# A decoder layer's projection stage with a third h buffer and norms ahead, and FFN norm sums moved from TensorE to GpSimd

## The chip, the cores and the metric

The kernel runs on the 8 cores of one Trainium2 chip, as one program on each. The metric is device time in microseconds (us) of the slowest core. A run is called slow when one die of four cores shows a lower granted TensorE clock and is over 1% longer than the other, or when it is over 1.5% above the fastest run of its kernel. Such runs happened to most kernels here (2755 to 3060 us) and are left out: all comparisons are of fast runs.

The four cores numbered 0 to 3 are die 0, the others die 1. Engines in the profile's words: PE is TensorE (PEld its weight loads), DVE is VectorE, ACT is ScalarE, POOL is GpSimd, SP is SyncE, whose queue issues most transfers. PSUM is the memory that TensorE writes its results to; another engine has to empty it. DMA stands for transfers.

## The reference

One layer: RMSNorm, one input projection, a convolution branch and a forgetting attention branch, a shared output projection, post-norm and residual, then a SwiGLU FFN with a norm before and behind it. Four sequences of 8192 tokens, width 1024, FFN width 2816.

```python
h = rmsnorm(x, g_mix_pre)
a_val, a_gate, q, k, v, f_logit = split(h @ w_in)
u = a_val * sigmoid(a_gate)                         # GLU, 512 channels
conv_out = silu(layernorm(causal_depthwise_conv(u, conv_w, conv_b)))   # width 31
log_f = log_sigmoid(f_logit + b_forget)
attn_out = forgetting_attention(q, k, v, log_f)     # causal, 8 heads x 64
mix = concat([conv_out, attn_out]) @ w_out
x = x + rmsnorm(mix, g_mix_post)
h = rmsnorm(x, g_ffn_pre)
y = (silu(h @ w_gate) * (h @ w_up)) @ w_down
x = x + rmsnorm(y, g_ffn_post)
```

Two cores share a sequence. Each computes k, v and forget logits for all 16 chunks of 512 tokens, and q, convolution, output and FFN for its own 8 chunks, the odd ones in its own numbering. Tensors are transposed: channels on partitions, tokens along the row.

## The kernel before

The program is written by Python generators. The "filler" (projection, then FFN) yields after every few matmuls; at each yield one deferred step of each waiting list is issued (`tick`), and a share of attention work is put in. In the traces each engine's work comes in the order written, so a matmul written ahead of another is also ahead of it there.

```python
# one buffer for all input weights; a part is a row block, so every load writes all 8 parts
win = BP("win", [128, 8, DIN], BF16, parts=8)
...
def wl(name, lo, hi, n=1):
    ...  # DMA with cast: out=win[:, :, lo:hi],
         # writes=[("winp", name)] + win.keys[...]   -> each load waits for the one before
wl("k", C_K, C_V); wl("v", C_V, DIN); wl("gv", 0, C_Q); wl("q", C_Q, C_K)
...
def p_chunk(i):                                      # (cut) one projection chunk
    own, j, H = i % 2 == 1, i // 2, hT[i % 2]        # two h buffers
    load_x(i + 1)
    K: 4 x 8 matmuls -> kst, deferred store to k_s;  V: 4 x 8 -> vst, deferred store to v_s
    squares of x(i+1) on ACT (deferred); forget logits
    if even:  conv_mm(j - 1), with norm_stats(i + 1) inside; conv_ln(j - 1)
    else:     Q; norm_stats(i + 1); gates: 4 x (GATE, VAL) -> u -> u_s in DRAM;
              then load u back as u4, four shifted copies (deferred)
    cvt_some(2)          # 2 of 30 conversions of FFN weights, DRAM to DRAM, f32 to bf16
...
def stats(src, nk, b, ...):                          # sum of squares over channels:
    nk matmuls of ones_bf by bf16 squares            # nk = 8 for every RMSNorm
def A2(j):                                           # norm behind the output projection
    yield from stats(sqf, 8, b); norm_tail(...)      # Ln and Exp on ACT give rstd
    defer("x1", [resid(mix, V_GPOST, X, ob) for ob in range(8)])       # DVE
    defer("x1", [square(X, sqf, ob) for ob in range(8)], 3)            # ACT
def A3(j):                                           # norm before the FFN
    flush("x1"); yield from stats(sqf, 8, b); norm_tail(...)
    defer("h2", [scale_by(x1[j % 2], V_GFPRE, rstdf, h2, k) for k in range(8)])
def N2(j): ...                                       # norm behind the FFN, same form
...
def f_stream():                                      # (cut) FFN; chunk j+1's norms inside chunk j
    f_load(0); f_loadx(0)
    A1(0); conv_mm(7); A2(0); conv_ln(7); A3(0); flush("ln")
    for j in range(8):
        11 up groups (32 matmuls each): N2(j-1) behind group 0; behind group 4, attention of
        chunk j+1 must be done; A1(j+1) behind groups 6 to 9
        8 down blocks (22 matmuls each): A2(j+1) ahead of block 0, A3(j+1) ahead of block 3
```

The softmax here doesn't subtract the row's maximum and nothing guards it: scores larger than these inputs give would overflow.

Of the kernel before, what the change touches and what calls it, by code (L numbers as in the profile page):

```python
# [10 lines left out]
D = 1024  # L11
# [182 lines left out]
def build_program():  # L194
# [66 lines left out]
    win = BP("win", [128, 8, DIN], BF16, parts=8)  # L261
    xs = BP("xs", [128, 8, CH], F32, parts=8)
    hT = [BP(f"hT{i}", [128, 8, CH], BF16, parts=8) for i in range(2)]
# [3 lines left out]
    rt = BP("rt", [128, CH], F32)  # L267
    rstd = BP("rstd", [128, CH], F32)
    w4 = BP("w4", [128, 8, 16, 32], BF16)
    u4 = BP("u4", [128, 16, WIN], BF16, planes=4)  # L270
    ust = [BP(f"ust{i}", [128, CH], BF16) for i in range(2)]
    th = [BP(f"th{i}", [128, CH], F32) for i in range(2)]
    acc = BP("acc", [128, 4, CH], F32, parts=4)
    lsq = BP("lsq", [128, 8, CH], BF16, parts=8)
    mean = BP("mean", [128, CH], F32)
    m2 = BP("m2", [128, CH], F32)
    lrt = BP("lrt", [128, CH], F32)
    lrs = BP("lrs", [128, CH], F32)
    lth = [BP(f"lth{i}", [128, CH], F32) for i in range(2)]
    cvst = [BP(f"cvst{i}", [128, CH], BF16) for i in range(2)]  # L280
    kmask = BP("kmask", [128, 4], F32)
# [3 lines left out]
    tot = BP("tot", [128, 32], F32)  # L285
# [6 lines left out]
    sq = BP("sq", [128, 8, CH], BF16, parts=8)  # L292

    fc = [base]
    BF_ = lambda name, shape, dt, parts=1: Buf(name, shape, dt, parts, fc)
    mix = BF_("mix", [128, 8, CH], F32, parts=8)
    x1 = [None, None]
    x1[0] = BF_("x1_0", [128, 8, CH], F32, parts=8)
    h2 = BF_("h2", [128, 8, CH], BF16, parts=8)
    fc[0] = max(fc[0], xs.off)  # L300
    at = BF_("at", [128, 4, CH], BF16)
    cv = BF_("cv", [128, 4, CH], BF16)
    sqf = BF_("sqf", [128, 8, CH], BF16, parts=8)
    fc[0] = max(fc[0], hT[0].off)
    wr = [BF_(f"wr{i}", [128, 2048], BF16) for i in range(NWR)]
    rtf = BF_("rtf", [128, CH], F32)
    rstdf = BF_("rstdf", [128, CH], F32)
    tmp = [BF_(f"tmp{i}", [128, CH], F32) for i in range(2)]
    actT = BF_("actT", [128, NFB, CH], BF16, parts=NFB)
    x1[1] = BF_("x1_1", [128, 8, CH], F32, parts=8)  # L310
    thf = [BF_(f"thf{i}", [128, CH], F32) for i in range(2)]
    sa = [BF_(f"sa{i}", [128, CH], F32) for i in range(2)]
    sqy = BF_("sqy", [128, 8, CH], BF16, parts=8)
    assert fc[0] <= sq.off
    fc[0] = max(fc[0], sq.off)
    wout = BF_("wout", [128, 8, D], BF16)
# [49 lines left out]
    def norm_tail(b, rtb, rstdb, scale, ncol=CH):  # L366
        P.op("act", lambda e: e.activation(out=rtb[:, 0:ncol], in_=pb[b][:, 0:ncol], func=AF.Ln, bias=epsb[:, 0:1], scale=scale),  # L367
             reads=[PB(b)] + epsb.keys, writes=rtb.keys)
        P.op("act", lambda e: e.activation(out=rstdb[:, 0:ncol], in_=rtb[:, 0:ncol], func=AF.Exp, scale=-0.5),
             reads=rtb.keys, writes=rstdb.keys)  # L370

    def stats(src, nk, b, ncol=CH, k0=0):
        yield from group(nk, lambda k: ones_bf[:], lambda k: src[:, k0 + k, 0:ncol], pb[b][:, 0:ncol],
                         lambda k: ones_bf.keys + [src.keys[k0 + k]], b, cost=ncol / 2400.0)
# [17 lines left out]
    def load_x(i):  # L392
        for g in range(4):
            ld("sp", xs, xs[:, 2 * g:2 * g + 2, :], xT_d[i, :, 2 * g:2 * g + 2, :], keys=xs.keys[2 * g:2 * g + 2], sem=("xs", g))

    def square(src, dst, k):
        return lambda: P.op("act", lambda e: e.activation(out=dst[:, k, :], in_=src[:, k, :], func=AF.Square),  # L397
                            reads=[src.keys[k]], writes=[dst.keys[k]])
# [6 lines left out]
    wkey = lambda k, c: [("winp", c)]  # L405

    def proj_T(H, c0, b, wk):
        yield from group(8, lambda k: win[:, k, c0:c0 + 128], lambda k: H[:, k, :], pb[b][:],
                         lambda k: [("winp", wk), win.keys[k], H.keys[k]], b)

    def norm_stats(i):
        b = bank()
        yield from stats(sq, 8, b)
        norm_tail(b, rt, rstd, 1.0 / D)
        defer("h", [scale_by(xs, V_GPRE, rstd, hT[i % 2], k) for k in range(8)], every=1)

    def c_chain(i, bf_):
# [6 lines left out]
        def part2():  # L424
            b = bank()
            mm(pb[b][:, 0:32], tri[:], lt[:], True, True, tri.keys + lt.keys, PB(b))
            mm(pb[b][:, 32:64], ones_f[:], lt[:], True, True, ones_f.keys + lt.keys, PB(b))
            P.op("dve", lambda e: e.tensor_copy(out=tot[:], in_=pb[b][:, 32:64]), reads=[PB(b)], writes=tot.keys)
            for tb in range(4):
                P.op("dve", lambda e, tb=tb: e.tensor_tensor(out=cc[:, tb, :], in0=pb[b][:, tb * 8:tb * 8 + 8], in1=carry[:], op=ALU.add),  # L430
                     reads=[PB(b)] + carry.keys, writes=cc.keys)
                P.op("dve", lambda e, tb=tb: e.tensor_tensor(out=carry[:], in0=carry[:], in1=tot[:, tb * 8:tb * 8 + 8], op=ALU.add),
                     reads=tot.keys + carry.keys, writes=carry.keys)
            if own:
                P.op("dve", lambda e: e.tensor_scalar(out=cs[:, 3, :], in0=cc[:].rearrange("p a h -> p (a h)"), scalar1=-1.0, scalar2=None, op0=ALU.mult),
                     reads=cc.keys, writes=cs.keys)
            src = cc
            if i == 0:
                P.op("dve", lambda e: e.tensor_tensor(out=cm[:], in0=cc[:], in1=kmask[:].unsqueeze(2).to_broadcast([128, 4, NH]), op=ALU.add),
                     reads=cc.keys + kmask.keys, writes=cm.keys)  # L440
                src = cm
            f = lambda a: a[:].rearrange("p a h -> p (a h)")
            P.op("dve", lambda e: e.tensor_copy(out=cs[:, 0, :], in_=f(src)), reads=src.keys, writes=cs.keys)
            P.op("dve", lambda e: e.tensor_tensor(out=f(c1), in0=f(src), in1=cs[:, 0, :], op=ALU.subtract),
                 reads=src.keys + cs.keys, writes=c1.keys)
            P.op("dve", lambda e: e.tensor_copy(out=cs[:, 1, :], in_=f(c1)), reads=c1.keys, writes=cs.keys)
            P.op("dve", lambda e: e.tensor_tensor(out=cs[:, 2, :], in0=f(c1), in1=cs[:, 1, :], op=ALU.subtract),
                 reads=c1.keys + cs.keys, writes=cs.keys)

        def part3():  # L450
            b = bank()
            mm(pb[b][:, 0:128], cs[:].rearrange("p a h -> p (a h)"), identb[:], True, True, cs.keys + identb.keys, PB(b))
            P.op("dve", lambda e: e.tensor_copy(out=cst[:], in_=pb[b][:, 0:128]), reads=[PB(b)], writes=cst.keys)
            st("sp", c_s[i].rearrange("a b h t -> (a b h) t"), cst[:], cst.keys, [("c_s", i)], "cst")
            ready[i] = True

        defer("c", [part2, part3], 4, 5)

    def conv_mm(j):
        for cb in range(4):  # L460
            b = bank()
            for k in range(8):
# [3 lines left out]
                if k == 3:  # L466
# [3 lines left out]
            P.op("act", lambda e, cb=cb: e.activation(out=lsq[:, 4 + cb, :], in_=acc[:, cb, :], func=AF.Square),  # L470
                 reads=[acc.keys[cb]], writes=[lsq.keys[4 + cb]])
            P.op("pool", lambda e, cb=cb: e.tensor_copy(out=lsq[:, cb, :], in_=acc[:, cb, :]),
                 reads=[acc.keys[cb]], writes=[lsq.keys[cb]])
            yield 16 * 0.057

    def conv_ln(j):
        b1 = bank()
        yield from stats(lsq, 4, b1)
        b2 = bank()
        yield from stats(lsq, 4, b2, k0=4)  # L480
# [4 lines left out]
        P.op("act", lambda e: e.activation(out=lrt[:], in_=m2[:], func=AF.Ln, bias=epsb[:, 0:1], scale=1.0), reads=m2.keys + epsb.keys, writes=lrt.keys)  # L485
        P.op("act", lambda e: e.activation(out=lrs[:], in_=lrt[:], func=AF.Exp, scale=-0.5), reads=lrt.keys, writes=lrs.keys)

        def steps(cb):
            A, AK = acc[:, cb, :], [acc.keys[cb]]
            L, C = lth[cb % 2], cvst[cb % 2]  # L490
# [11 lines left out]
            def three():  # L502
                P.op("dve", lambda e: e.scalar_tensor_tensor(out=C[:], in0=L[:], scalar=1.0, in1=A, op0=ALU.add, op1=ALU.mult),
                     reads=AK + L.keys, writes=C.keys)
                st("sp", conv_s[cb * 128:(cb + 1) * 128, j * CH:(j + 1) * CH], C[:], C.keys, [("conv_s", j, cb)], C.name)
# [3 lines left out]
        defer("ln", [fs[0][0], fs[1][0], fs[0][1], fs[1][1], fs[2][0], fs[0][2], fs[1][2], fs[3][0], fs[2][1], fs[3][1], fs[2][2], fs[3][2]], 2)  # L509
# [10 lines left out]
    def halo():  # L520
# [4 lines left out]
        norm_tail(b, lrt, lrs, 1.0 / D, HN)  # L525
# [5 lines left out]
    def halo_mm():  # L531
        xh, hh, sqh, uh = u4h
        for cb in range(4):
            b = bank()
            for o, c0 in ((0, C_GATE + cb * 128), (HN, C_VAL + cb * 128)):
                yield from group(8, lambda k: win[:, k, c0:c0 + 128], lambda k: hh[:, k, :], pb[b][:, o:o + HN],
                                 lambda k: [("winp", "gv"), win.keys[k]] + hh.keys, b, cost=HN / 2400.0)
# [533 lines left out]
```

## Time and profile before

| | before |
|---|---|
| median of four runs | 2713.73 us (2711.61 to 2798.83, which is slow; the three fast ones end at 2714.15) |
| span of the profiled cores | 2686.6 to 2717.8 us, granted clock 0.962 to 0.968 |
| PE / ACT / DVE / POOL busy | 89% / 59% / 36% / 5% |

The head of the page of the slowest core, busy time of each engine:

```profile
span 2717.8 us, 53428 instructions; the slowest of 8 cores (2686.6 to 2717.8 us)
## 1 busy us (share of the span) xinstructions
PE 2410.2 (89%) x19531; PEld 1236.3 (45%) x19864; DVE 989.3 (36%) x1731; ACT 1602.9 (59%) x1957; POOL 127.6 (5%) x331
```

There are 19864 weight loads and 19531 matmuls, yet every matmul has its load: 333 matmul records are missing. The busy time of PE therefore can't be compared closely between two kernels. The Trainium skill warns of the same row for another reason (Perfetto Trace Analysis, Identifying the Most-Contended Engine: matmul busy share is no good measure of the distance to the roofline, because matmuls are pipelined).

This document uses another measure, **loss**: time less matmul work. Work is counted from the weight loads, each taken at the columns of its matmul over 2.4 per ns: 0.213 us for 512 columns, a quarter of it where four convolution matmuls share the array. Those of 65 and of 8 columns are taken at 0.033 us, an estimate: in this trace the 65-column ones start 0.029 to 0.036 us apart. (Trainium skill, TensorE: Matmul & The Clock Gate, "Wait — 56ns, not 53.3ns?": start to start is N over 2.4 GHz plus 2.5 ns when warm. The last row below agrees: 49.74 us by 228 is 0.218 us; the median start to start of the 512-column matmuls on this core is 0.216.) Loss holds waits, lower clock and all else. The kernel before has 2327 us of work and 391 us of loss on the slowest core.

Busy time in stretches of 50 us, then granted clock, DMA share, GB/s:

```profile
core 2: us, PE busy (x) PEld busy (x) DVE busy (x) ACT busy (x) POOL busy (x), PEclk, DMA share, GB/s
0.00:50.00 50.00, 4.68 (x8) 0.83 (x8) 12.37 (x21) 15.44 (x27) 3.27 (x9) 1.00 0.86 171
...
750.00:800.00 50.00, 40.86 (x373) 22.19 (x382) 12.94 (x23) 32.09 (x40) 3.77 (x10) 0.94 0.81 164
1050.00:1100.00 50.00, 27.50 (x207) 11.96 (x210) 30.06 (x46) 27.44 (x37) 1.23 (x2) 0.73 0.31 93
1350.00:1400.00 50.00, 49.57 (x411) 26.23 (x416) 14.21 (x22) 32.04 (x39) 1.13 (x4) 1.00 0.65 193
...
2600.00:2650.00 50.00, 49.74 (x228) 22.70 (x232) 19.52 (x29) 8.96 (x15) 0.00 (x0) 1.00 0.50 157
```

The start, the projection and the change to the FFN (1050 us) have gaps, and in the last two the clock is down too (0.94 and 0.73; the 1.00 of the first row says nothing, since this core's clock records begin at 73.7 us). The FFN is nearly full. The waits of TensorE up to 1016 us, longest in total first (us in total, times, longest):

```profile
PE pbig L356 <- DMA s_win<-w_in: 45.7, 1, 45.7
PE pbig L356 <- DMA s_u_82<-u_s: 24.7, 4, 9.9
...
PE pbig L356 <- DMA s_kr_53<-c_s: 10.5, 1, 10.5
```

That is one wait of 45.7 us for the input weights, four for u to come back from DRAM, and one for a few KB of forget sums beside the keys (29 us with two more of its kind). These are the waits that the change aims at.

### The profile page before, as it was taken

How to read it: one execution, taken by the hardware profiler on the slowest of the kernel's cores; microseconds unless marked ns; L12 is line 12 of the kernel's file. 1: busy time of each engine (PE TensorE's matmuls, PEld its weight loads, DVE VectorE, ACT ScalarE, POOL GpSimd, SP SyncE). 2: the span in 40 equal slices, each digit the busy share in tenths (PEclk: the TensorE clock that was granted, in tenths of full speed). 3: DMA queues.
4: the chain of work that ended last, by engine and by line, in shares of the span. 5: the costliest groups of instructions: out<-in, count | busy, mean ns of one | idle time of the engine just before them, and what ended most of it. 6: DMA issues, size and time to landing. Idle time of an engine off the chain costs nothing.

```text
span 2717.8 us, 53428 instructions; the slowest of 8 cores (2686.6 to 2717.8 us)
## 1 busy us (share of the span) xinstructions
PE 2410.2 (89%) x19531; PEld 1236.3 (45%) x19864; DVE 989.3 (36%) x1731; ACT 1602.9 (59%) x1957; POOL 127.6 (5%) x331
## 2 busy tenths in 40 slices
PE   0777978989988976999999999999999999999997
PEld 0433434445444433554555554545445455454443
DVE  1425343443535424323324323242332332334443
ACT  2153656667767646667667666666666666673221
POOL 0010110010100100000000000000000000000000
PEclk9988989989999988999999999999999999999998
DMA  8364746567577655443553552463455355345443
GB/s 158 90 141 104 159 114 152 126 162 159 132 145 152 139 134 125 143 137 105 169 166 98 170 181 84 137 202 92 122 157 154 103 162 171 92 137 193 130 157 106
DMA packets 219708, 377.65 MB, mean 139 GB/s; under 512 B 36576, under 2 KB 146400, under 8 KB 217568
## 3 DMA queue, kind: packets, MB, share of 16 engines
q1 hardware_dynamic: 213920, 349.52, 46.2%
q0 software_dynamic: 5536, 24.69, 5.9%
q8 instruction: 167, 2.74, 0.4%
q14 instruction: 85, 0.70, 0.1%
HBM read 347.57 MB, written 68.55 MB: 153 GB/s over the span
## 4 chain that ended last, share of the span: by engine, by line
PE 69%; DVE 10%; DMA 7%; ACT 7%; issue 5%; SPq 2%; POOL 0%; DVEq 0%; ACTq 0%; POOLq 0%
PE pbig L356 69%; DMA s_win<-w_in 2%; DMA s_u_82<-u_s 2%; DMA u_s<-s_ust_84 1%; SPq L328 1%; DVE s_tmp_123 L699 1%; DVE s_tmp_124 L699 1%; DVE s_x_1_126 L701 1%; ACT s_pt_60 L879 1%; DVE s_x_0_110 L701 1%; ACT s_pt_59 L879 1%; ACT s_pt_61 L879 1%; ACT s_pt_62 L879 1%; ACT L367 1%; DMA conv_s<-s_cvst_95 1%
## 5 line engine op out<-in xcount | busy, mean ns | idle before, releaser
L879 ACT ACTIVATE s_pt_59<-pbig 128x1024 bf16<-128x1024 f32 x288 | 294.4, 1022 | 224.8 <-PE pbig L356 223.0
L879 ACT ACTIVATE s_pt_60<-pbig 128x1024 bf16<-128x1024 f32 x288 | 294.4, 1022 | 152.3 <-PE pbig L356 150.3
L879 ACT ACTIVATE s_pt_61<-pbig 128x1024 bf16<-128x1024 f32 x288 | 294.3, 1022 | 134.6 <-PE pbig L356 132.8
L879 ACT ACTIVATE s_pt_62<-pbig 128x1024 bf16<-128x1024 f32 x224 | 229.0, 1023 | 170.8 <-PE pbig L356 168.9
L356 PE MATMUL pbig<-s_hT_75,s_win 128*128 128x512 bf16 x972 | 265.4, 395 | 41.0 <-DVE s_hT_75 L401 15.7
L356 PEld LDWEIGHTS pbig<-s_hT_75,s_win 128*128 128x128 bf16 x1024 | 94.8, 100 | 146.4 <-issue 60.4
L884 POOL TENSOR_SCALAR_AFFINE_SELECT s_pt_61<-s_pt_61 128x128 bf16<-128x128 bf16 x192 | 62.7, 326 | 2084.1 <-ACT s_pt_61 L879 2046.6
L743 DVE SCALAR_TENSOR_TENSOR s_sa_129<-s_thf_127,pbig 128x512 f32<-128x512 f32 x88 | 60.4, 687 | 251.6 <-ACT s_thf_127 L742 242.4
L743 DVE SCALAR_TENSOR_TENSOR s_sa_130<-s_thf_128,pbig 128x512 f32<-128x512 f32 x88 | 60.5, 687 | 245.4 <-ACT s_thf_128 L742 237.8
L770 DVE COPY s_mix<-pbig 128x512 f32<-128x512 f32 x64 | 44.1, 690 | 241.1 <-PE pbig L356 241.1
L356 PE MATMUL pbig<-s_h_111,s_wr_115 128*128 128x512 bf16 x445 | 115.6, 382 | 16.9 <-DVE s_h_111 L401 12.1
L356 PE MATMUL pbig<-s_h_111,s_wr_118 128*128 128x512 bf16 x459 | 117.3, 378 | 1.9 <-DVE s_sa_130 L743 0.8
L356 PE MATMUL pbig<-s_h_111,s_wr_120 128*128 128x512 bf16 x444 | 115.9, 385 | 3.2 <-DVE s_sa_129 L743 1.5
L356 PE MATMUL pbig<-s_h_111,s_wr_117 128*128 128x512 bf16 x456 | 116.0, 378 | 2.4 <-DVE s_actT L747 1.1
L356 PE MATMUL pbig<-s_h_111,s_wr_116 128*128 128x512 bf16 x439 | 113.4, 379 | 3.4 <-DVE s_sa_130 L743 2.1
L356 PE MATMUL pbig<-s_h_111,s_wr_119 128*128 128x512 bf16 x443 | 113.0, 378 | 1.5 <-DVE s_actT L747 0.5
L356 PE MATMUL pbig<-s_hT_74,s_win 128*128 128x512 bf16 x243 | 64.4, 389 | 46.4 <-DMA s_win<-w_in 45.7
L356 PE MATMUL pbig<-s_u_82,s_w_81 128*32 128x512 bf16 x1024 | 73.5, 413 | 24.7 <-DMA s_u_82<-u_s 24.7
L397 ACT ACTIVATE s_sq<-s_xs 128x512 bf16<-128x512 f32 x128 | 73.9, 622 | 30.2 <-DMA s_xs<-xT 30.1
L771 ACT ACTIVATE s_sqy<-s_mix 128x512 bf16<-128x512 f32 x64 | 40.1, 627 | 81.5 <-DVE s_mix L770 81.5
L719 DVE COPY s_mix<-pbig 128x512 f32<-128x512 f32 x64 | 44.3, 692 | 118.0 <-PE pbig L356 118.0
L742 ACT ACTIVATE s_thf_128<-pbig 128x512 f32<-128x512 f32 x88 | 52.2, 593 | 51.5 <-PE pbig L356 51.5
(235 smaller groups left out, 4395.9 us busy)
## 6 DMA issues: line engine op xcount, KB each, us to landing
s_xs<-xT SPq DMA_DIRECT2D x60, 512.0 KB, 8.0
s_u_82<-u_s SPq DMA_DIRECT2D x32, 540.0 KB, 9.6
s_wr_117<-wg_b SPq DMA_DIRECT2D x30, 512.0 KB, 4.2
s_wr_118<-wu_b SPq DMA_DIRECT2D x30, 512.0 KB, 5.2
s_wr_115<-wg_b SPq DMA_DIRECT2D x29, 512.0 KB, 4.2
s_wr_116<-wu_b SPq DMA_DIRECT2D x29, 512.0 KB, 4.7
s_wr_119<-wg_b SPq DMA_DIRECT2D x29, 512.0 KB, 4.4
s_wr_120<-wu_b SPq DMA_DIRECT2D x29, 512.0 KB, 5.2
```

The costliest lines, as they stand in the source:

```text
L328: P.dma(q, lambda e: e.dma_start(out=out, in_=in_), reads=reads, writes=keys, sem=sem or buf.name)
L356: P.op("pe", lambda e: e.matmul(out, lhsT=lhsT, rhs=rhs, start=start, stop=stop, **kw), reads=reads, writes=[wkey])
L397: return lambda: P.op("act", lambda e: e.activation(out=dst[:, k, :], in_=src[:, k, :], func=AF.Square), reads=[src.keys[k]], writes=[dst. ...
L699: P.op("dve", lambda e: e.tensor_tensor(out=T[:], in0=src[:, ob, :], in1=rstdf[:], op=ALU.mult), reads=[src.keys[ob]] + rstdf.keys, writes ...
L701: P.op("dve", lambda e: e.scalar_tensor_tensor(out=X[:, ob, :], in0=T[:], scalar=V(goff + ob), in1=X[:, ob, :], op0=ALU.mult, op1=ALU.add) ...
L719: P.op("dve", lambda e, b=b, ob=ob: e.tensor_copy(out=mix[:, ob, :], in_=pb[b][:]), reads=[PB(b)], writes=[mix.keys[ob]])
L742: P.op("act", lambda e: e.activation(out=T[:], in_=pb[bg][:], func=AF.Tanh, scale=0.5), reads=[PB(bg)], writes=T.keys)
L743: P.op("dve", lambda e: e.scalar_tensor_tensor(out=A[:], in0=T[:], scalar=1.0, in1=pb[bg][:], op0=ALU.add, op1=ALU.mult), reads=T.keys + [ ...
L770: P.op("dve", lambda e: e.tensor_copy(out=mix[:, ob, :], in_=pb[b][:]), reads=[PB(b)], writes=[mix.keys[ob]])
L771: P.op("act", lambda e: e.activation(out=sqy[:, ob, :], in_=mix[:, ob, :], func=AF.Square), reads=[mix.keys[ob]], writes=[sqy.keys[ob]])
L879: P.op("act", lambda e: e.activation(out=p[:], in_=pbig[:, 2 * s:2 * s + 2, :], func=AF.Exp), reads=[PB(2 * s), PB(2 * s + 1)], writes=p.keys)
L884: sel = lambda e, ap: e.affine_select(out=ap, in_=ap, pattern=[[1, 128]], base=0, channel_multiplier=-1, compare_op=ALU.is_ge, fill=0.0)
```

## The change

The intent: keep TensorE fed in the projection, and take the norm sums of the FFN off it.

1. Weights in three buffers (k and v apart as well), so K waits for its own load only.
2. A third h buffer. The norm of the next chunk is finished inside K or V of this one, the convolution of an own chunk runs one own chunk later, u is loaded back two chunks ahead of it, small stores and ring loads are issued some steps later, the short forget-sum steps go to GpSimd, and attention starts 8 us of filler after its inputs are ready.
3. The last chunk's gates move into the first norms of the FFN; the last convolution into the first FFN chunk.
4. FFN norms: ScalarE squares in f32, GpSimd adds the eight up, splits the sum into a bf16 value and a bf16 rest, and TensorE needs 2 ones-matmuls instead of 8. There are 24 such norms.
5. Conversions of FFN weights go from 2 a chunk to 3 a chunk, from chunk 2.

The diff, cut to its core (buffer placement and renamings left out):

```diff
-    win = BP("win", [128, 8, DIN], BF16, parts=8)
+    winKV = BP("winKV", [128, 8, 1032], BF16, planes=2)
+    winQ = BP("winQ", [128, 8, 512], BF16)
+    winG = BP("winG", [128, 8, 1024], BF16)
-    hT = [BP(f"hT{i}", [128, 8, CH], BF16, parts=8) for i in range(2)]
+    hT = [BP(f"hT{i}", [128, 8, CH], BF16, parts=8) for i in range(3)]
...
+    def sq_pair(src, k, first, ss):          # one: ACT square into sqr; two: POOL ss += sqr
+    ...
+    def split(ss, hl):
+        P.op("pool", lambda e: e.tensor_copy(out=hl[:, 0, :], in_=ss[:]), ...)
+        P.op("pool", lambda e: e.tensor_tensor(out=hl[:, 1, :], in0=ss[:], in1=hl[:, 0, :], op=ALU.subtract), ...)
...
     def p_chunk(i):
+            if not own and i > 0 and hp == 1:        # inside K
+                yield from norm_fin(i + 1)
...
+                if tb == 0:                          # inside V of an own chunk
+                    norm_sq(i + 1)
+                if tb == 3:
+                    yield from norm_fin(i + 1)
+            if not own and i > 0 and tb == 3 and i + 2 < NCH:
+                flush("h")
+                load_x(i + 2)
...
+        if not own and j > 0:                        # end of an even chunk
+            load_u(j - 1)
...
+            if j > 0:                                # own chunk, behind Q
+                yield from conv_mm(j - 1)
-        cvt_some(2)
+        if i > 1:
+            cvt_some(3)
...
     def A2(j):
-        yield from stats(sqf, 8, b)
+        flush("sqm")
+        yield from stats(hlA, 2, b)
...
-        defer("x1", [square(X, sqf, ob) for ob in range(8)], 3)
+        defer("x1", sq_steps(X, 8, ssA, hlA), 4)
...
     def f_stream():
-        yield from A1(0, range(8))
-        yield from conv_mm(NOWN - 1)
-        yield from A2(0)
-        yield from conv_ln(NOWN - 1)
-        yield from A3(0)
-        flush("ln")
+        yield from A1(0, range(8))
+        yield from gates(J, 0, H)
+        yield from conv_ln(J - 1)
+        flush("ln")
+        yield from A2(0)
+        for cb in (1, 2, 3):
+            yield from gates(J, cb, H)
+        yield from A3(0)
...
+            t0 = fa[0]                               # attention, at each query chunk
+            while fa[0] < min(t0 + 8.0, p_end[0]):
+                yield None
```

## The prediction

> **What bounds the kernel now.** TensorE. The page has PE busy 2410 of 2718 us (89%), granted clock 0.964. Counted from the code, the matmuls are 2327 us at full clock, so about 390 us are lost: 307 us idle and 83 us of lower clock. By stretches:
>
> - 0 to 200 us: 95 us idle, 8 us of clock.
> - 200 to 1000 us (projection): 106 us idle, 47 us of clock.
> - 1000 to 1100 us (change of stage): 27 us idle, 17 us of clock (0.73 at 1050 to 1100).
> - 1100 to 2450 us (FFN with attention): only 50 us idle, 15 us of clock.
>
> The clock falls where TensorE idles, as the Trainium skill has it (TensorE: Matmul & The Clock Gate, Part 1): a gap is paid for twice.
>
> The waits by stretch: the first matmul waits 45.7 us for input weights, because four loads write one buffer one after another (20+18+16+12 us in the chain) and K waits for the last; u from DRAM 24.7 us; c for keys 29 us; squares and h about 35 us; at the change of stage h2 12 us, squares 10 us.
>
> **What the change does.**
>
> 1. Three weight buffers: K starts at about 33 us instead of 69. DMA then binds (0.86 busy in the first 50 us). Estimate: 40 us saved.
> 2. Norms ahead, third h buffer, conv a chunk later, stores and ring loads issued later: the named waits mostly go. I assume 200 to 400 us recovers 30 us, and 400 to 1000 us falls from 63 us idle and 30 us of clock to a little above the FFN's level (50 us saved).
> 3. The last gates fill the first FFN norms, the last conv moves into chunk 0: 30 us of 44 saved. h2 of chunk 0 is still flushed at once, so 5 to 10 us remain. The output weights load later, just in time.
> 4. FFN norm sums: 8 ones-matmuls become 2, three norms in eight chunks: 144 matmuls of 512 columns, 0.213 us each = 31 us off the bounding engine, nearly all critical.
>
> Added: GpSimd does 7 adds, a cast and a subtract per norm. The trace has 0.78 us for a 128x512 cast there; the Trainium skill (GPSIMD Engine Reference, Elementwise — side-by-side cycle accounting) gives 4.5 us for a 2048-wide add, so I estimate 1.2 us for 512: 10 us a norm, 240 us in all on an engine 5% busy. They spread over 13 of 18 steps between A2 and A3, so should not bind; at the kernel's end they add about 3 us. ACT is unchanged (59%).
>
> Sum: 40+80+30+31 = about 180 us.
>
> **Prediction: 2540 us, range 2475 to 2625.** Faster by over 2%: 0.92; within 2%: 0.06; slower: 0.02.
>
> **What would show it.** First K matmul near 33 us; waits for u and c almost gone; PE at 45 or more of each 50 us from 400 us on, clock near 1.00; FFN starting 130 us earlier; the FFN's ones-matmuls down from 192 to 48; POOL busy 350 to 400 us; FFN idle no higher than now.
>
> **What would make it wrong.** Total DMA may bind the start, so freeing K only moves the wait to x, Q or gates. The attention's extra 8 us delay may leave early projection without work to fill gaps. GpSimd latency, or its contention with VectorE, may open new waits before A3. Output weights landing late may stall A1.

## The result

The kernel after takes 2677.66 us (median of four runs, 2674.63 to 2684.99), all fast. The ratio to before is 0.9874 (95% interval 0.9847 to 0.9900): 1.3% faster, where 6.4% was predicted. That is within the 2% to which the prediction had given a chance of 0.06. Ratios here are the mean time of one kernel's fast runs over that of the other's of the same rounds, so they differ a little from the ratio of the medians quoted.

The head of the page after. PE busy is the same in us, in part for the reason given above; POOL is at 433 us:

```profile
span 2674.4 us, 54150 instructions; the slowest of 8 cores (2653.0 to 2674.4 us)
...
PE 2410.8 (90%) x19720; PEld 1224.2 (46%) x19720; DVE 988.6 (37%) x1530; ACT 1601.4 (60%) x1959; POOL 433.3 (16%) x748
```

Work and loss by stage, medians of the eight cores, worked out as told above. "Chunk 14 to A1" ends at the first matmul with the output weights, "A1 to up" at the first FFN matmul, "FFN alone" begins where the attention has ended.

| stage | loss before | loss after | change | predicted |
|---|---|---|---|---|
| start to chunk 2 | 93 | 70 | -24 | -40 |
| chunks 2 to 13 | 128 | 121 | -8 | about -80 |
| chunk 14 to A1 | 26 | 8 | -18 | in the next row |
| A1 to up | 29 | 32 | +3 | -30 with the row above |
| FFN with attention | 70 | 85 | +15 | 0 |
| FFN alone | 31 | 49 | +19 | 0 |
| all loss | 378 | 365 | -13 | -150 |
| matmul work | 2327 | 2297 | -31 | -31 |

The sum, -44 us, is the change of the median span (2707.4 to 2662.8). Three things stand out: the steady projection hardly gained, the change of stage as a whole gave 15 us of 30, and the FFN gave back, as loss, all that the 144 matmuls had saved.

How far can a row be trusted? The kernels e1, e6, e7, f1, f2 and f3 below have the projection of after unchanged. Counted again from the traces, their medians for chunks 2 to 13 lie 1 to 10 us above that of after, and the cores of one run differ there by some 30 us. (This second count gives 3 to 4 us more in that row for nearly every kernel, and as much less for FFN with attention; the differences between kernels are the same.) So the 8 us by which chunks 2 to 13 gained are within the scatter, and so is any difference under some 10 us in that row. The other rows repeat far better: from A1 on, the cores of one run mostly agree within 5 us.

Stretches of 50 us of the kernel after, same columns as before:

```profile
250.00:300.00 50.00, 36.89 (x330) 19.59 (x328) 16.41 (x30) 23.20 (x27) 6.29 (x20) 0.90 0.96 170
400.00:450.00 50.00, 34.37 (x268) 17.65 (x268) 12.99 (x25) 21.35 (x29) 3.77 (x17) 0.80 0.82 172
950.00:1000.00 50.00, 32.58 (x258) 16.15 (x254) 28.66 (x39) 35.00 (x43) 12.18 (x11) 0.86 0.29 98
...
2450.00:2500.00 50.00, 41.63 (x193) 18.68 (x191) 28.12 (x36) 15.94 (x25) 19.81 (x16) 0.95 0.30 87
```

In the first two the transfer engines are busy 0.96 and 0.82 of the time. The third is the change of stage, the fourth the FFN after the attention has ended, with POOL busy.

What TensorE waits for up to 935 us, the end of the projection in the kernel after:

```profile
PE pbig L353 <- DVE s_vst L678: 25.3, 5, 12.0
...
PE pbig L353 <- DVE s_tot L465: 14.2, 2, 11.8
...
PE pbig L353 <- DVE s_kst L663: 11.6, 3, 6.1
```

The waits for u and for weights are gone. In their place TensorE waits for VectorE to empty PSUM into the staging buffers of v and k. VectorE itself waits, in the same stretch:

```profile
DVE s_vst L678 <- DMA v_s<-s_vst: 48.9, 5, 17.9
...
DVE s_kst L663 <- DMA k_s<-s_kst: 32.1, 3, 16.7
```

That is 81 us for the store of the chunk before to leave the one staging buffer. In before these two lines don't exist. One such wait in the chain of the kernel after, between 160 and 200 us (start, duration):

```profile
164.55 0.70 DVE s_vst L678
...
165.31 27.59 DMA v_s<-s_vst
...
193.06 0.70 DVE s_vst L678
```

The store of 0.5 MB takes 27.6 us to land; the median of its kind is 7.6 us. Issued just ahead of it are 2 MB of x, just behind it 2.2 MB of u and, 3 to 5 us later, three conversions of FFN weights.

### The profile page after: what moved, and what is told of

The parts are those of the page before. It is cut to its first block, busy times and chain, and to the rows that moved or that the text cites. A ratio compares the mean times of both kernels' runs of the same rounds, so it can differ in the third digit from the quotient of the medians.

```text
span 2674.4 us, 54150 instructions; the slowest of 8 cores (2653.0 to 2674.4 us)
## 1 busy us (share of the span) xinstructions
PE 2410.8 (90%) x19720; PEld 1224.2 (46%) x19720; DVE 988.6 (37%) x1530; ACT 1601.4 (60%) x1959; POOL 433.3 (16%) x748
## 4 chain that ended last, share of the span: by engine, by line
PE 68%; DVE 8%; SPq 7%; ACT 7%; DMA 6%; issue 4%; POOL 1%; DVEq 0%; ACTq 0%; POOLq 0%
PE pbig L353 68%; SPq L325 6%; DVE s_tmp_96 L772 1%; DVE s_x_1_117 L774 1%; DMA v_s<-s_vst 1%; DVE s_tmp_95 L772 1%; DMA k_s<-s_kst 1%; DVE s_x_0_116 L774 1%; DMA s_xs<-xT 1%; DMA s_kr_51<-c_s 1%; DMA s_kr_49<-c_s 1%; ACT s_pt_61 L966 1%; ACT s_pt_60 L966 1%; ACT L365 1%; DMA s_kr_52<-c_s 1%
## 5 line engine op out<-in xcount | busy, mean ns | idle before, releaser
L353 PE MATMUL pbig<-s_h_120,s_wr_121 128*128 128x512 bf16 x464 | 121.8, 388 | 3.8 <-DVE s_h_120 L434 3.5
L353 PE MATMUL pbig<-s_h_120,s_wr_124 128*128 128x512 bf16 x480 | 122.4, 381 | 0.9 <-DVE s_sa_130 L817 0.9
L353 PE MATMUL pbig<-s_h_120,s_wr_122 128*128 128x512 bf16 x464 | 118.7, 382 | 4.4 <-DVE s_sa_130 L817 4.4
L353 PE MATMUL pbig<-s_h_120,s_wr_123 128*128 128x512 bf16 x480 | 122.2, 381 | 0.0
L389 POOL TENSOR_TENSOR s_ssA<-s_ssA,s_sqr_98 128x512 f32<-128x512 f32 x56 | 76.2, 1361 | 281.0 <-ACT s_sqr_98 L383 278.8
L353 PE MATMUL pbig<-s_h_120,s_wr_126 128*128 128x512 bf16 x464 | 117.4, 378 | 2.2 <-DVE s_sa_129 L817 1.5
L389 POOL TENSOR_TENSOR s_ssA<-s_ssA,s_sqr_97 128x512 f32<-128x512 f32 x56 | 76.9, 1373 | 257.4 <-ACT s_sqr_97 L383 254.7
L353 PE MATMUL pbig<-s_h_120,s_wr_125 128*128 128x512 bf16 x464 | 117.4, 378 | 0.0
L678 DVE CAST s_vst<-pbig 128x512 bf16<-128x512 f32 x64 | 44.1, 690 | 113.3 <-PE pbig L353 63.9
L816 ACT ACTIVATE s_th_94<-pbig 128x512 f32<-128x512 f32 x88 | 52.2, 593 | 47.1 <-PE pbig L353 47.1
L353 PE MATMUL pbig<-s_sq,s_ones_bf 128*128 128x512 bf16 x192 | 53.6, 400 | 24.5 <-ACT s_sq L444 17.4
L816 ACT ACTIVATE s_th_93<-pbig 128x512 f32<-128x512 f32 x88 | 52.2, 594 | 35.2 <-PE pbig L353 30.1
```

The costliest lines, as they stand in the source:

```text
L353: P.op("pe", lambda e: e.matmul(out, lhsT=lhsT, rhs=rhs, start=start, stop=stop, **kw), reads=reads, writes=[wkey])
L389: P.op("pool", lambda e: e.tensor_tensor(out=ss[:], in0=ss[:], in1=d[:], op=ALU.add), reads=ss.keys + d.keys, writes=ss.keys)
L678: P.op("dve", lambda e, b=b, tb=tb: e.tensor_copy(out=vst[:, :, tb, 0:64], in_=pb[b][:].rearrange("p (h d) -> p h d", h=NH)), reads=[PB(b) ...
L816: P.op("act", lambda e: e.activation(out=T[:], in_=pb[bg][:], func=AF.Tanh, scale=0.5), reads=[PB(bg)], writes=T.keys)
```

## The experiments

Eighteen kernels were run. Each is the kernel after with the edit shown, but for one that edits before. The ratios are to before; after itself has 0.9874.

### Where the FFN's saving went

**e1: sums back on TensorE.**

```diff
-            defer("sqm", list(sq_pair(mix, ob, ob == 0, ssA)) + [lambda: split(ssA, hlA)] * (ob == 7))
+            P.op("act", ... out=sqf[:, ob, :], in_=mix[:, ob, :], func=AF.Square ...)
-        yield from stats(hlA, 2, b)
+        yield from stats(sqf, 8, b)          # the same in A3, and with sq in N2
```

> The kernel after, with the FFN norm sums back on TensorE (8 ones-matmuls of bf16 squares for each norm). Theory: the GpSimd sums save 31 us of matmuls and give about as much back in waits, 15 us while attention runs and 19 us when FFN is alone. Then the loss (time less matmul work) of FFN with attention falls from 85 to about 70 us and of FFN alone from 49 to about 31 us, and the time is within 10 us of after (2665 to 2685). Rival: the sums are worth their 31 us, and the FFN's extra loss comes from elsewhere (gates and conv moved in, attention later): then about 2705 us, with the FFN's losses as in after.

Measured: 2684.11 us, ratio 0.9862 (0.9843 to 0.9882), as after. The FFN's loss went from 85 + 49 to 68 + 35 us, 32 us less, for 31 us more work. Within the intervals the GpSimd sums as built are worth nothing.

**e6: the norms with little or no attention beside them on TensorE, 20 of 24 left on GpSimd.**

```diff
+        yield from (stats(sqf, 8, b) if j >= 7 else stats(hlA, 2, b))     # A2, A3
+        yield from (stats(sq, 8, b) if j >= 6 else stats(hlA, 2, b))      # N2
```

> The kernel after, with the four norms that fall where little or no attention is left (both norms before the FFN of the last chunk, the norms behind the FFN of the last two) on TensorE as in before, the other 20 on GpSimd. Theory: where nothing fills TensorE, the chain square, add, cast, subtract shows as a wait; then the loss of FFN alone falls from 49 to about 33 us for 5 us of matmuls more, and the ratio to before from 0.987 to about 0.983 (11 us). Rival: the 49 us are not the GpSimd chain; then the loss stays and the time grows by 5 us.

Measured: 2673.44 us, ratio 0.9844 (0.9824 to 0.9865). FFN alone lost 33 us instead of 49, as expected; FFN with attention stayed at 82. The waits of TensorE from 2450 us on show the same. First before, then after:

```profile
PE pbig L356 <- DVE s_actT L747: 3.7, 3, 1.6
```

```profile
PE pbig L353 <- POOL s_hlA L405: 12.9, 2, 8.9
```

The line of after is the cast near the end of the GpSimd chain, waited for by a ones-matmul with nothing left to fill the time.

**f1: which of the three norms.** Only the norm behind the FFN of chunks 0 to 6, and both norms of chunk 0, stay on GpSimd.

```diff
+        yield from (stats(sq, 8, b) if j > 0 else stats(hlA, 2, b))       # A2, A3
+        yield from (stats(sq, 8, b) if j == NOWN - 1 else stats(hlA, 2, b))   # N2
```

> The kernel after; on GpSimd stay only the norms behind the FFN of chunks 0 to 6 and both norms of chunk 0; the two norms before the FFN of chunks 1 to 7 and the very last norm go back to TensorE (90 matmuls, 19 us). Theory: only the sums between A2 and A3, and those with nothing beside them, cost more than they save; then the stretch of the first three down blocks loses about 4 us a chunk less beside attention and 18 us less in the last chunks; FFN loss falls by 45 us in all for 19 us of matmuls: ratio about 0.978. Rival: every norm on GpSimd costs the same; then the ratio is about 0.986.

Measured: two fast runs of four, 2663.63 and 2692.27 us. In the profiled run (2663.63) the FFN's loss is 55 + 33 us instead of 85 + 49: 46 less, for 19 us of matmuls. The loss by place, chunks 0 to 6 together (us):

| | before | after | e1 (all on TensorE) | f1 |
|---|---|---|---|---|
| first half of the up groups (norm behind the FFN) | 28 | 27 | 35 | 23 |
| down blocks 0 to 2 (between A2 and A3) | 32 | 56 | 22 | 24 |
| last chunk, from down block 3 to the end | 21 | 26 | 21 | 21 |

So the norm behind the FFN is well placed on GpSimd: its sum has time, and nothing is lost for it. The two norms before the FFN are not: A2's result is needed for x, whose squares are needed for A3 three down blocks later. At the very end the chain costs 5 us more. The first row is not pure: chunk 0 has no such norm, and chunk 7 has one. Over chunks 1 to 7 it is 31, 22, 29 and 17 us, counted again, which says the same more clearly.

**f2: is it GpSimd slowing VectorE?** VectorE's residual steps in the kernel after, in order of time, while GpSimd begins to add at 2065.56 us:

```profile
2064.61 0.68 DVE L772 TENSOR_TENSOR s_tmp_95<-s_mix,s_rstd 128x512 f32<-128x512 f32 x1
2065.40 0.75 DVE L774 SCALAR_TENSOR_TENSOR s_x_1_117<-s_tmp_95,s_vecs,s_x_1_117 128x512 f32<-128x512 f32 x1
2066.07 1.76 DVE L772 TENSOR_TENSOR s_tmp_96<-s_mix,s_rstd 128x512 f32<-128x512 f32 x1
2067.93 1.57 DVE L774 SCALAR_TENSOR_TENSOR s_x_1_117<-s_tmp_96,s_vecs,s_x_1_117 128x512 f32<-128x512 f32 x1
```

The same operation takes 0.68 us alone and 1.76 us beside an add on GpSimd. On all eight cores of this run, 832 of these operations had no such add beside them and took 0.68 to 0.78 us; the 192 that had one took 1.75 us in the median. The Trainium skill (GPSIMD Engine Reference, Specifications) says that GpSimd shares its SBUF interfaces with VectorE and contends with VectorE instructions that have two SBUF inputs; this trace agrees, and gives the size. ScalarE, in order, then waited for x with exponentials of the attention behind it. The edit lets the squares, and with them the adds, start later:

```diff
-        defer("x1", sq_steps(X, 8, ssA, hlA), 4)
+        defer("x1", sq_steps(X, 8, ssA, hlA), 8)
```

> The kernel after, with the squares of the new x before the FFN starting 4 steps later (step 8 instead of 4); all sums stay on GpSimd. Theory: GpSimd's adds slow VectorE's residual operations (0.68 to 1.7 us where they overlap), so ScalarE, in order, waits for x with exponentials behind it; with the squares later the residuals run mostly alone (mean of the odd ones from 0.94 to 0.8 us or less) and the loss of the first three down blocks falls from 8 to 6 us a chunk: 8 to 15 us faster than after. Rival: the chain's length before A3 is what counts; then a later start makes it worse, 5 us or more.

Measured: 2694.18 us, ratio 0.9904 (0.9885 to 0.9923), 8 us slower than after by the ratio, with intervals that overlap. The theory fell, in a telling way. Most of the contention went: groups of operations, VectorE's first residual step, in after (one of its two buffers; the other's 64 have a mean of 719 ns) and then in f2 (both buffers together; busy us, mean ns):

```profile
L772 DVE TENSOR_TENSOR s_tmp_96<-s_mix,s_rstd 128x512 f32<-128x512 f32 x64 | 60.2, 940 | 0.0
```

```profile
L772 DVE TENSOR_TENSOR s_tmp<-s_mix,s_rstd 128x512 f32<-128x512 f32 x128 | 89.4, 698 | 59.1 <-ACT s_rstd L367 59.1
```

But the loss of down blocks 0 to 2 stayed at 56 us and that of the blocks behind A3 rose from 3 to 9. Without contention the later chain costs as much or more, so the length of the chain before A3 is enough to make the loss. How the 4 us a chunk in after divide between the slower VectorE and the chain stays open.

### The projection

**e2: two staging buffers each for k and v**, chunks taking turns, in memory that only the FFN uses.

```diff
+    kst = [kst, OV("kst1", [128, 4, CH], BF16, sqr[0], 4, 4160)]
+    vst = [vst, OV("vst1", [128, NH, 4, 65], BF16, sqr[0])]
...
+        KS, VS = kst[i % 2], vst[i % 2]
```

> The kernel after, with two staging buffers each for k and v, chunks taking turns. Theory: in after the k and v stores land late behind the x and u loads; with one staging buffer VectorE, in order, waits for them (81 us by its waits in the projection, 0 in before) and TensorE waits for VectorE. Then those waits go, the loss of chunks 2 to 13 falls from 121 us to 95 or less, and the time is 2640 to 2655 us. Rival: the transfers themselves bound the projection; then TensorE waits for x, u or keys instead, and the time stays within 8 us of after (2677).

Measured: 2686.22 us, ratio 0.9872 (0.9852 to 0.9891): no gain. VectorE's waits for k and v stores are gone, and the loss of chunks 2 to 13 is 131 us, within the scatter of after. What TensorE waits for between 130 and 935 us is now (in after the first of these waits was 15 us in all):

```profile
PE pbig L356 <- DMA s_kr<-c_s: 45.2, 6, 17.4
...
PE pbig L356 <- DMA s_u<-u_s: 8.4, 1, 8.4
```

The wait moved from late stores to late loads of a few KB beside the keys. The staging buffer was where the delay showed, not what made it. My theory lost to its rival.

**e9: u in another queue.**

```diff
-            ld("sp", u4, u4[32 * s:32 * s + 32, :, :],
+            ld("pool", u4, u4[32 * s:32 * s + 32, :, :],
```

> The kernel after, with the loads of u issued on GpSimd's queue instead of SyncE's; nothing else moved. Theory: what stalls the projection is the order in one queue, small stores and key loads landing behind u's 2.2 MB; with u in another queue VectorE's waits for the k and v stores fall from 73 us to under 30 and the loss of chunks 2 to 13 from 121 to 100 or less. Rival: the 16 transfer engines are full in these bursts whatever queue feeds them; the waits shift but the loss stays above 112 us.

Measured: three fast runs, 2693.76 to 2716.68 us, ratio 0.9941 (0.9887 to 0.9995): 18 us slower than after by the ratios. VectorE still waited 66 us for v stores in the profiled core, and the loss of chunks 2 to 13 rose to 145. The Trainium skill lets one expect no gain (DMA: Bandwidth & Descriptors, Issuing engines are not separate DMA queues): transfers of all issuing engines run on the same 16 DMA engines and interleave. This run agrees that another queue does not help; whether the rise comes from GpSimd's own work for its queue was not tried.

**e10: fewer conversions, wrong result.**

```diff
+    cvt = [cvt[0], cvt[1], cvt[22]]
...
-            wseq.append((wg_b[fg]..., ("wg_b", fg), 2048))
+            wseq.append((wg_b[0]..., ("wg_b", 0), 2048))     # the same for wu_b, wd_b
```

> Wrong result on purpose: the kernel after with 3 of the 30 weight conversions (DRAM to DRAM); every FFN group reads the first group's weights, so shapes, matmuls and FFN loads stay. Theory: the volume of transfers in the projection is what bounds it; without about 45 MB of conversion traffic the loss of chunks 2 to 13 falls from 121 to 80 us or less and the time by 40 us or more (ratio 0.972 or less). Rival: latency and order, not volume; then the loss stays at 105 us or more.

Measured: two fast runs, 2647.13 and 2639.61 us, ratio 0.9718 (0.9690 to 0.9746), 42 us faster than after by the ratios. The loss of chunks 2 to 13 fell from 121 to 85 us, all else as in after. VectorE's waits for the store of v between 100 and 935 us fell to this, and none for k is left; in after they were 49 and 24 us in that stretch:

```profile
DVE s_vst L679 <- DMA v_s<-s_vst: 17.2, 1, 17.2
```

So the conversions hold the projection up. The edit also spares GpSimd 27 issues of about 0.5 us each, which no run separates from the transfers.

**e4: conversions at the old rate.**

```diff
-        if i > 1:
-            cvt_some(3)
+        if i > 0:
+            cvt_some(2)
```

> The kernel after, with 2 FFN weight conversions (DRAM to DRAM) a chunk from chunk 1, as before had, instead of 3 a chunk from chunk 2. If the larger bursts of conversion are what delays stores, loads of u and keys: 10 to 25 us faster (2652 to 2667). If not: within 5 us of after (2672 to 2682).

Measured: 2674.75 us against 2721.11 for before on this chip, ratio 0.9838 (0.9821 to 0.9855), 10 us better than after by the ratios, with intervals that just overlap. Chunks 2 to 13 lose 108 us instead of 121, chunk 14 loses 15 instead of 8. The larger bursts of the change cost part of what its other edits gained here.

**f4: the conversion volume moved, right result.** 22 conversions go at 1 or 2 a chunk, the 8 of the down weights into the first FFN chunk.

```diff
-        if i > 1:
-            cvt_some(3)
+        if i > 0 and len(cvt) > 8:
+            cvt_some(2 if own else 1)
...
+                if j == 0 and fg < 8:
+                    cvt_some(1)
```

> The kernel after, with the 22 conversions of gate and up weights spread 1 or 2 a chunk over the projection and the 8 of the down weights moved into the first FFN chunk; right result. If volume in the projection's bursts is what costs: the loss of chunks 2 to 13 falls from 121 to about 95 us, the FFN's loss stays, ratio about 0.978. If moving only shifts the cost into the FFN: ratio 0.984 or more.

Measured: 2659.8 us, ratio 0.9774 (0.9752 to 0.9795), 27 us better than after by the ratios. Chunks 2 to 13 lose 82 us, as little as with hardly any conversions at all; the FFN gives back 10, chunk 14 gives back 5. Set beside e4 and e10 this narrows the cause: 3, 2 and about 1.5 conversions a chunk go with 121, 108 and 82 us of loss, and 3 in all with 85. In these runs it is how much falls into one chunk that costs, rather than the total: 22 of the 30 are still in the projection here.

**e3: u later.**

```diff
-        if not own and j > 0:
-            load_u(j - 1)
+            if own and j > 0 and hp == 3:
+                load_u(j - 1)
```

> The kernel after, with the load of u issued after K of the odd chunk instead of at the end of the even chunk, right behind x and the v store. Theory: it is the u load beside the x load that delays the stores; then VectorE's waits for k and v stores fall from 81 to under 40 us and the time by 10 to 25 us (2652 to 2667). Rival: u comes too late for the conv, which waits some us each time, and the time is as after or longer (2675 to 2695).

Measured: three fast runs, 2668.71 to 2679.45 us, ratio 0.9833 (0.9806 to 0.9859), 11 us better than after by the ratios, with intervals that overlap; chunks 2 to 13 lose 111 us. The time is as expected, but the waits are not: VectorE still waits 65 us for k and v stores in the profiled core between 100 and 935 us (73 in after), where under 40 was expected. Moving u away from x may help by some us; it is not the sole cause.

**e5: without the attention's delay.**

```diff
-            t0 = fa[0]
-            while fa[0] < min(t0 + 8.0, p_end[0]):
-                yield None
```

> The kernel after, without the attention's delay of 8 us of other work at each new query chunk. If the delay leaves TensorE without work to fill gaps, the loss of chunks 2 to 13 falls by 5 to 15 us. If the delay covers the landing of keys, waits for keys grow and the time is 5 to 15 us longer than after.

Measured: two fast runs, 2686.94 and 2689.71 us, ratio 0.9899 (0.9874 to 0.9924), some 7 us slower than after by the ratios, with overlapping intervals; the loss of chunks 2 to 13 is 130, within the scatter. So the delay does no harm that shows; that it helps is not shown.

### The start

**b1: the kernel before, with the weight loads tracked as four parts.** Nothing else is changed.

```diff
-    win = BP("win", [128, 8, DIN], BF16, parts=8)
+    win = BP("win", [128, 8, DIN], BF16, planes=4)
...
-                      writes=[("winp", name)] + win.keys[ks[0]:ks[-1] + 1], ...
+                      writes=WP[name], ...
```

> The kernel before, with one change alone: the four loads of the input weights are tracked as four parts of the buffer, so that they need not land one after another and K waits for its own. Prediction on record: K starts at about 33 us and about 40 us are saved. The kernel after saved 24 us of loss by chunk 2. Theory: total transfer then binds, so the start saves 15 to 30 us (ratio 0.989 to 0.994). Rival (the prediction): 35 us or more, ratio 0.987 or less.

Measured: ratio 0.9947 (0.9921 to 0.9974), fast runs from 2699.63 to 2726.21 us. The loss up to chunk 2 fell from 93 to 69 us, what the whole change reached, so this one edit is enough for the gain at the start. But chunks 2 to 13 then lost 137 us instead of 128, and of 24 us about 14 remained. The profiled run had die 0 at a clock of 0.945 against 0.960 on die 1, within the limits of a fast run. On die 1 alone, counted again, chunks 2 to 13 lose 138 to 145 us, against 125 to 135 in before: most of the later loss is there too, though near the scatter.

### The change of stage

**e7: two gates ahead of the forced finish of the layer norm.**

```diff
         yield from conv_ln(J - 1)
+        yield from gates(J, 1, H)
+        yield from gates(J, 2, H)
         flush("ln")
         yield from A2(0)
...
-        for cb in (1, 2, 3):
-            yield from gates(J, cb, H)
+        yield from gates(J, 3, H)
```

> The kernel after, with two of the last gates ahead of the forced finish of the conv's layer norm at the change of stage, where after has one gap of 12.6 us with ScalarE as the releaser. Theory: the forced finish puts VectorE and ScalarE steps in a row ahead of the attention's exponentials; with the steps spread over the gates the loss from A1 to the first up matmul falls from 32 to about 20 us, ratio about 0.983. Rival: with less work left between the two norms the same time is waited there: within 3 us of after.

Measured: one fast run of five, 2690.95 us. In its profile the loss from A1 to up is 36 us instead of 32: the gap moved to the next norm, where TensorE waits 19.9 us for the cast of the GpSimd chain. As far as one profile tells, the rival had it.

**f3: scratch of its own for that layer norm**, so it need not be finished by force.

```diff
-        yield from conv_ln(J - 1)
-        flush("ln")
+        yield from conv_ln(J - 1, sa)
         yield from A2(0)
...
         for cb in (1, 2, 3):
             yield from gates(J, cb, H)
+        flush("ln")
```

> The kernel after, with separate scratch for the layer norm that is still running at the change of stage, so that it need not be finished by force before A2 and trickles between the gates. If the forced finish, 16 us of VectorE and ScalarE steps ahead of the exponentials, makes the 12.6 us gap: the loss from A1 to the first up matmul falls from 32 to 20 us or less, ratio about 0.983. If the gap only moves to the next norm, as when the gates were moved: within 4 us of after.

Measured: 2677.92 us, ratio 0.9849 (0.9830 to 0.9868), at best 7 us better than after, with overlapping intervals. The loss from A1 to up is 27 us instead of 32, more than the 20 expected. The forced finish is a part of this loss. The GpSimd sums of the two norms are another: e1, which put them back on TensorE, loses 26 us here (24 to 29 on every core, against 31 to 33 in after). The rest stays open.

**e8: attention spread further into the FFN.**

```diff
-    A_END, R_MAX = 0.86, 1.1
+    A_END, R_MAX = 0.93, 1.1
```

> The kernel after, with the attention spread to 0.93 of the other work instead of 0.86, so that the last chunk's norms before its FFN have attention beside them. Theory: FFN alone is 37 us shorter in work for each 0.025 moved, and its loss falls from 49 to about 30 us, since only the last norm is left bare; time 8 to 15 us shorter. Rival: GpSimd's latency shows beside attention too; then the loss moves to FFN with attention and the time stays within 4 us.

Measured: 2752.7 us, ratio 1.0111 (1.0073 to 1.0149): slower than before. FFN alone began at the same matmul as in after, because attention of the last chunk must be done before A1(7). The attention that had been put off had to run there with no filler, and the loss of FFN with attention went from 85 to 134 us. My expectation overlooked that limit.

### Parts together

**e12: e3, e4 and e6 together.**

> The kernel after with u loaded after K of the odd chunk, two conversions a chunk from chunk 1, and the last norms on TensorE. Alone they gave 11, 10 and 8 us. If the first two help for separate reasons: 25 to 30 us faster than after, ratio about 0.977. If both ease the same bursts: 15 to 20 us, ratio about 0.981.

Measured: two fast runs of four, 2642.45 and 2654.16 us (before: 2718.7 median of the fast runs). Chunks 2 to 13 lose 82 us. Both edits on bursts together gave 39 us of loss, more than 10 and 13 alone.

**g1: f4, e3, f1 and f3 together.**

> The kernel after with four edits together: conversions spread (22 in the projection, 8 in the first FFN chunk), u loaded after K of the odd chunk, sums before the FFN back on TensorE, scratch of its own for the layer norm at the change of stage. If the losses are separate they add: 27 us from conversions, 27 us from the sums, 5 us from the scratch, 0 to 10 us from u: 2610 to 2620 us, ratio about 0.962. If they overlap: 0.968 or more.

Measured: three fast runs, 2615.72 to 2623.74 us, ratio 0.9629 (0.9604 to 0.9654). The parts add up: chunks 2 to 13 lose 77 us, A1 to up 28, the FFN 64 + 33.

**g2: g1 and the two staging buffers of e2.**

> g1 with two staging buffers each for k and v. If VectorE's waits for late k and v stores still bind once the bursts are smaller: 5 to 15 us faster than g1. If the transfers bind whatever waits for them: within 4 us of g1.

Measured: 2608.81 us, all four runs fast, ratio 0.9595 (0.9578 to 0.9611): 4.1% faster than before and 2.8% faster than after, result correct. The second staging buffer, worth nothing alone, is worth 9 us by the ratios once the bursts are smaller (the intervals of g1 and g2 just overlap): start to chunk 2 and chunks 2 to 13 lose 7 us less each. The head of its page:

```profile
span 2604.9 us, 53488 instructions; the slowest of 8 cores (2581.6 to 2604.9 us)
...
PE 2387.5 (92%) x19479; PEld 1229.2 (47%) x19810; DVE 963.9 (37%) x1531; ACT 1598.8 (61%) x1957; POOL 266.2 (10%) x613
```

## Why the prediction was wrong

It expected 2540 us (2475 to 2625) and faster by over 2% at 0.92. The measured 2677.66 us lies outside. The direction held, and the readings of before held; what failed was the step from a wait removed to time gained, in the projection above all, and the claim that the GpSimd sums would not bind. The count of matmuls was right.

1. "Three weight buffers … 40 us saved": 24 us of loss. The mechanism was right. The first K matmul started at 24 us, earlier than the 33 foretold, and b1 shows that this edit alone makes the gain. The rest went, as its own warning had it, into new waits: with all loads at once the DMA share is 1.00 in the first 50 us, and before 150 us TensorE waits 11.8 us for the staging buffer of u and 6.1 us for that of k, against 0 and 1.2 in before.

2. "The named waits mostly go … 30 us" and "50 us saved": 8 us. This is the step that failed most. The named waits mostly did go (for u from 24.7 us to none, for forget sums beside keys from 29 to 15). What failed is the inference that their time would be gained. They were treated as separate causes, and in the kernel after they prove to be places where late transfers show. There the lateness shows at the k and v staging buffers (81 us of VectorE waits), and with those doubled at the key loads (45 us of TensorE waits). Taking conversions away (e10) or spreading and moving them (f4) took 36 to 39 us off the loss; giving it another place to be waited for, or another queue, took off nothing. The profile of before already showed a DMA share of 0.39 to 0.83 in these stretches, 0.81 in the row at 750 us. And the change itself moved against it: conversions in bursts of 3 instead of 2, u loaded right behind x, and the same bytes (378 MB in all). With the conversions back at 2 a chunk (e4) the loss is 108 us: so the other edits gained some 20 us of the 128, and the bursts of 3 took some 13 back. What makes up the 70 to 82 us that are left in g2 and f4 is not known.

3. "The last gates fill the first FFN norms … 30 us of 44 saved": 15 us. The 18 us before the first output matmul were gained; from there to the first up matmul 3 us were lost. A layer norm finished by force put a row of VectorE and ScalarE steps ahead of the attention's exponentials. f3 shows 5 us of that, and e1 some 6 us for the GpSimd sums in these two norms; the rest of the 32 us is not explained.

4. "144 matmuls … 31 us off the bounding engine, nearly all critical": the work did fall by 31 us, and the FFN's loss rose by 34. "They spread over 13 of 18 steps between A2 and A3, so should not bind" failed. The operations were sized fairly (1.15 to 1.37 us an add or subtract, against an estimate of 1.2; POOL busy 433 us, against 350 to 400). Their cost is not POOL's occupancy but a chain of square, add, cast and subtract in front of a matmul that TensorE comes to in order. f1 shows where it binds: between A2 and A3, and where no attention is left. "At the kernel's end they add about 3 us": 5. "FFN idle no higher than now": higher.

The warnings listed at the end of the prediction named total DMA, though only for the start, and GpSimd latency before A3; all outcomes short of 2% faster were given 0.08, and these warnings deserved the main place. The warning about the attention's delay is not borne out: e5, without the delay, is no faster. The output weights were in time: no wait for them is among TensorE's waits.

## What to carry to other kernels

When several waits on transfers end in different places, first ask what their transfers share: remove volume in one experiment, with a wrong result if need be, and spread it in another, before you reorder buffers and queues. A longer chain on an idle engine is free only where its result has slack: count the steps between the last input and the matmul that needs it, also for the chunk that has nothing beside it. An edit that seems worthless alone, such as a second staging buffer, may pay once the larger limit is gone, so try it again in the end.

## What the Trainium skill lacked or had wrong

- GPSIMD Engine Reference: it names the contention with VectorE instructions that have two SBUF inputs, but neither it nor SBUF — State Buffer gives a duration for such a pair of operations. Here a 128x512 f32 VectorE operation went from 0.68 to 1.76 us beside a GpSimd add, and the adds had means of 1.29 to 1.37 us; two with VectorE idle took 1.27, and those beside it up to 1.72.
- DMA: Bandwidth & Descriptors: nothing was found wrong; that another issuing queue does not help was confirmed (e9: ratio 0.9941 against 0.9874). I found no figure in it for how late a transfer lands in the middle of a burst: here a store of 0.5 MB with a median of 7.6 us took 27.6 us.
- No page that I read tells that neighbouring cores differ in such a kernel. In the profiled run of after, one core of each pair (0 and 1, 2 and 3, and so on) is 16 to 21 us longer than the other (2653.0 and 2674.4, 2670.7 and 2654.8), with the median loss of chunks 2 to 13 at 121 us and a range of 110 to 142. Why was not tried.
